# Block totals at the blocks' first positions, and one empty step moved behind level 32, in a gated recurrence on one Trainium2 core

## The chip, the core and the metric

The kernel runs on one core of a Trainium2 chip. The engines of the core have short names in the profile: PE is TensorE, which does the matrix products (PEld is its loading of weights), DVE is VectorE, ACT is ScalarE, POOL is GpSimd, and SP is SyncE, which issues most of the DMAs. The metric is the device time of one execution in microseconds (us), lower is better, as the median of several runs.

## The reference

One layer with a gated linear recurrence (HGRN2), followed by an MLP with a squared ReLU, on 1024 tokens of width 1024 in fp32. The recurrence has 8 heads of width 128. For every head, with gates f, keys k, values v and queries q that come out of one projection:

```python
def step(S, t):                 # S is 128x128 per head
    S = f[t][:, None] * S + k[t][:, None] * v[t][None, :]
    return S, S.T @ q[t]        # o[t]
k = (1 - lb) * sigmoid(-proj_f);  f = lb + (1 - lb) * sigmoid(proj_f)
q = silu(proj_q) / sqrt(128)
x = x + (rmsnorm_per_head(o) * gain * silu(proj_g)) @ w_out
x = x + relu(rmsnorm(x) @ w1) ** 2 @ w2;  out = rmsnorm(x)
```

The reference itself computes the recurrence in chunks of 64 positions, from sums of log f.

## The kernel before

**The products.** Each fp32 operand is split into a high and a low part, and a product of two tiles is three matmuls (L209, L210, L211: high by high, high by low, low by high) that accumulate in PSUM. I call these three a triple. The projections are made for a pair of column blocks at a time by a scheme with seven products in place of eight, from sums of blocks of weights (tiles w..s, split by ACT at L162 and DVE at L163). For each head h there is a `pair` for q and f (j = 0) and one for v and g (j = 1). The last head's second pair is followed by the output projection, whose operands are loaded and split by `fetch` (L805 to L813, with the split at L782 on ACT and L783 on DVE).

**The recurrence in levels.** Within a block of 128 positions the kernel uses no running product in time. It goes by doubling: at level m (1, 2, 4, ..., 64) neighbouring blocks of m positions are joined. The scores between a query of the right block and a key of the left block are a matmul of k and q, which up to then have been multiplied with the gates inside their own blocks. After the matmul of a level three multiplications on DVE carry the tiles to the next level: `carry_q` (L387) multiplies q of the right block with the total gate of the left one, `carry_k` (L394) multiplies k of the left block with the total of the right one, and `carry_f` (L401) makes the total of the joined block. q, k and f are tiles of 128 x 1024; a multiplication touches half of q or k (512 columns), and of f 512 columns at level 1, 256 at level 2, 128 at level 4, and so on.

**The units.** A head's recurrence is a list of steps (L765): `small` (levels 0, 1 and 2: L568, 32 matmuls that read the tile qd made by `prefixes`), `middle` (levels 4 and 8: L601, 32 matmuls that read the tile qe made by `prefixes_2`), `leaf` (level 16: L619), `big` for 32 and for 64 (L649), then kt, vt, kv (the state), `o_unit` (the output, L706 and L708), z (its norm, ACT at L712 and L718), `zt` (transposes, L755) and sums for the output projection. `None` in the list is an empty step. The masked scores are copied out of PSUM by DVE (copy_predicated, L579 to L583 for `small`, L610 for `middle`).

**What sets the order.** The order on PE is the order in which the program is written. In `pair`, after every triple, `pump(650.0)` adds 650 to an account, and whenever that holds `SPACING` (1730, or `LAST_SPACING`, 1800, from the last head's second pair on) the next step of the list is written there, so steps stand two or three triples apart. On DVE, ACT, POOL and SP the tile framework's scheduler sets the order in this part of the program, with a higher priority for the steps of the recurrence (`ahead`: 150, and 400 for the last head). Each engine then works its list in order. The tags in `LEFT` and `NEXT` (L817 to L826) say in which buffers the operands of the output projection are put, and so which earlier use must be over; the key of `LEFT` is the product of the last pair after which they are fetched.

Of the kernel before, what the change touches and what calls it, by code (L numbers as in the profile page):

```python
# [25 lines left out]
ALU = mybir.AluOpType  # L26
# [3 lines left out]
P = 128  # L30
# [9 lines left out]
LEVELS = (1, 2, 4, 8, 16, 32, 64)  # L40
LEAF = 32
SPACING = 1730.0
LAST_SPACING = 1800.0
AHEAD = 6
WARM = 36
WARM_ROW = (6, 6, 6, 4)
# [3 lines left out]
def trunk(ctx: ExitStack, tc: tile.TileContext, x, gains, masks, gfin, w_in, w_out, w1, w2, out):  # L50
    nc = tc.nc
# [197 lines left out]
    with tc.tile_pool(name="scan", bufs=1) as sp:  # L249
# [134 lines left out]
        def halves(a, m):  # L384
            return a.rearrange("p (n two m) -> p n two m", two=2, m=m)

        def carry_q(q, f, m):  # L387

            n = T // (2 * m)
            te = halves(f, m)[:, :, 0, m - 1:m]  # L390
            qo = halves(q, m)[:, :, 1, :]
            nc.vector.tensor_tensor(qo, qo, te.to_broadcast([P, n, m]), ALU.mult)  # L392

        def carry_k(k, f, m):  # L394

            n = T // (2 * m)
            to = halves(f, m)[:, :, 1, m - 1:m]
            ke = halves(k, m)[:, :, 0, :]
            nc.vector.tensor_tensor(ke, ke, to.to_broadcast([P, n, m]), ALU.mult)  # L399

        def carry_f(f, m):  # L401

            fv = halves(f, m)
            te, to = fv[:, :, 0, m - 1:m], fv[:, :, 1, m - 1:m]
            nc.vector.tensor_tensor(to, te, to, ALU.mult)  # L405

        shapes = {"q": ([P, T], 2), "qd": ([P, T // LEAF, 80], 1), "k": ([P, T], 1), "f": ([P, T], 1),
                  "vT": ([P, T], 1), "sg": ([P, T], 1)}
# [128 lines left out]
        def prefixes(tl):  # L537


            q, f, qd = tl["q"], tl["f"], tl["qd"]  # L540
            qb = q.rearrange("p (n l) -> p n l", l=LEAF)
            nc.vector.tensor_tensor(qb, qd[:, :, :LEAF], f.rearrange("p (n l) -> p n l", l=LEAF), ALU.mult)
            nc.scalar.activation(qd[:, :, 32:48], qb[:, :, 1::2], AF.Copy)
            carry_q(q, f, 1)
            q4 = q.rearrange("p (n b j) -> p n b j", b=8, j=4)
            f4 = f.rearrange("p (n b j) -> p n b j", b=8, j=4)
            x1 = qd[:, :, 48:64].rearrange("p n (b j) -> p n b j", j=2)
            x0 = qd[:, :, 64:80].rearrange("p n (b j) -> p n b j", j=2)
            nc.scalar.activation(x1, q4[:, :, :, 2:4], AF.Copy)
            nc.vector.tensor_tensor(x0, q4[:, :, :, 2:4], f4[:, :, :, 1:2].to_broadcast([P, 32, 8, 2]), ALU.mult)  # L550

        def scan_units(h, tl):

# [6 lines left out]
            def small():  # L560
                pss = []
                for g in range(2):
                    ps = psum.tile([P, 4, 80], F32, name=f"lv{h}_0_{g}", tag="s")
                    pss.append(ps)
                    for j in range(4):
                        for b in range(P // LEAF):
                            n = (4 * g + j) * 4 + b
                            nc.tensor.matmul(ps[b * LEAF:(b + 1) * LEAF, j, :], k[:, n * LEAF:(n + 1) * LEAF],  # L568
                                             tl["qd"][:, n, :], start=True, stop=True)
                carry_k(k, f, 1)  # L570
                carry_f(f, 1)
                carry(2)
                prefixes_2()
                m0, m1, m2, m3 = (mk[:, i:i + 1, :] for i in range(4))
                m2, m3 = (m.rearrange("p c (b j) -> p c b j", j=4) for m in (m2, m3))
                for g, ps in enumerate(pss):
                    ac = Ac[:, 4 * g:4 * g + 4, :]
                    a4 = ac.rearrange("p c (b j) -> p c b j", j=4)
                    nc.vector.copy_predicated(ac, m0.to_broadcast([P, 4, LEAF]), ps[:, :, :LEAF])  # L579
                    nc.vector.copy_predicated(ac[:, :, 1::2], m1[:, :, 1::2].to_broadcast([P, 4, 16]), ps[:, :, 32:48])  # L580
                    for i, mm in enumerate((m2, m3)):
                        pv = ps[:, :, 48 + 16 * i:64 + 16 * i].rearrange("p c (b j) -> p c b j", j=2)
                        nc.vector.copy_predicated(a4[:, :, :, 2:4], mm[:, :, :, 2:4].to_broadcast([P, 4, 8, 2]), pv)  # L583

            def prefixes_2():


                qe = st["qe"] = sp.tile([P, T // LEAF, 80], F32, name=f"qe{h}", tag="qd", bufs=1)
                q8 = q.rearrange("p (n b j) -> p n b j", b=4, j=8)
                nc.scalar.activation(qe[:, :, :16].rearrange("p n (b j) -> p n b j", j=4), q8[:, :, :, 4:8], AF.Copy)  # L590
                carry_q(q, f, 4)
                q16, f16 = (a.rearrange("p (n b j) -> p n b j", b=2, j=16) for a in (q, f))
                x1, x0 = (qe[:, :, c:c + 16].rearrange("p n (b j) -> p n b j", j=8) for c in (16, 32))
                nc.scalar.activation(x1, q16[:, :, :, 8:16], AF.Copy)
                nc.vector.tensor_tensor(x0, q16[:, :, :, 8:16], f16[:, :, :, 7:8].to_broadcast([P, 32, 2, 8]), ALU.mult)

            def middle():
                ps = psum.tile([P, NC, 48], F32, name=f"lv{h}_4", tag="s")
                for n in range(T // LEAF):
                    c, b = n // 4, n % 4  # L600
                    nc.tensor.matmul(ps[b * LEAF:(b + 1) * LEAF, c, :], k[:, n * LEAF:(n + 1) * LEAF],  # L601
                                     st["qe"][:, n, :48], start=True, stop=True)
                carry_k(k, f, 4)
                carry_f(f, 4)
                carry(8)
                for i, j, lo in ((4, 4, 0), (5, 8, 16), (6, 8, 32)):
                    odd = [a.rearrange("p c (b two j) -> p c b two j", two=2, j=j)[:, :, :, 1, :]
                           for a in (Ac, mk[:, i:i + 1, :])]
                    pv = ps[:, :, lo:lo + 16].rearrange("p c (b j) -> p c b j", j=j)
                    nc.vector.copy_predicated(odd[0], odd[1].to_broadcast([P, NC, 16 // j, j]), pv)  # L610
                free("qd")

            def leaf(m, i):
                def run():
                    ps = psum.tile([P, NC, LEAF], F32, name=f"lv{h}_{m}", tag="s")
                    for c in range(NC):
                        for b in range(P // LEAF):
                            s = slice(c * P + b * LEAF, c * P + (b + 1) * LEAF)
                            nc.tensor.matmul(ps[b * LEAF:(b + 1) * LEAF, c, :], k[:, s], q[:, s],  # L619
                                             start=True, stop=True)  # L620
                    carry(m)
                    nc.vector.copy_predicated(Ac, mk[:, i:i + 1, :].to_broadcast([P, NC, LEAF]), ps)  # L622
                    if m == LEAF // 2:
                        for b in range(P // LEAF):
                            r = slice(b * LEAF, (b + 1) * LEAF)
                            nc.scalar.activation(AT[r, :, r], Ac[r, :, :], AF.Copy)  # L626
                return run

            def carry(m):

                carry_q(q, f, m)
                carry_k(k, f, m)
                if m == 64:
                    tot = st["tot"] = sp.tile([P, NC], F32, name=f"tot{h}", tag="tot", bufs=2)
                    fv = halves(f, m)
                    nc.vector.tensor_tensor(tot, fv[:, :, 0, m - 1], fv[:, :, 1, m - 1], ALU.mult)
                else:
                    carry_f(f, m)

# [76 lines left out]
            def z_unit():  # L716
                for c in range(NC):
                    nc.scalar.activation(st["z"][:, c, :], st["o"][c // 4][:, c % 4, :], AF.Copy,  # L718
                                         scale=st["r"][:, c:c + 1])
# [29 lines left out]
            def zt():  # L749

                z = tl["sg"]
                for a in range(2):
# [9 lines left out]
                    elif h < last:  # L762
                        nc.sync.dma_start(z_d[h][:, o], z[:, o])

            return (([None] * 4 + [small] + [None] * 2 if h == 0 else [None] * 2 + [small, None, None]) + [middle, None, leaf(16, 7), None]  # L765
                    + [big(32), big(64), None, kt, ("values", h), vt, kv, None, o_unit, lambda: (z_unit(), sums_load()), None, zt, sums_make])

# [35 lines left out]
        def fetch(keys, tags, stages):  # L805

            for i in range(0, len(keys), 2):
# [8 lines left out]
        OPS = [operands(i) for i in range(7)]  # L816
        LEFT = {"b": (OPS[0], ("hT00", "hT01", "hT02", "hT03", "hT04", "hT05"), ("m0", "m1", "m8")),  # L817
                "s2": (OPS[1][:4], ("d4", "d5", "d6", "d7"), ("hT07", "m9")),
                "s1": (OPS[1][4:], ("d0", "d1"), ("m2",)),
                "d": (OPS[2], ("d2", "d3", "d8", "d9", "d10", "d11"), ("m3", "m0", "m1"))}  # L820

        NEXT = {0: (OPS[3], ("hT14", "hT15", "hT16", "hT17", "hT10", "hT11"), ("m2", "m3", "m0")),
                1: (OPS[4], ("hT12", "hT13", "hT00", "hT01", "hT02", "hT03"), ("m1", "m2", "m3")),
                2: (OPS[5] + [("z", 1, 6)], ("hT04", "hT05", "d4", "d5", "d6", "d7", "d10"), ("m0", "m1", "m2", "m3")),
                3: ([("w", 0, 6), ("w", 0, 7), ("w", 1, 6), ("w", 1, 7)] + OPS[6],
# [328 lines left out]
    small = {}  # L1154
# [228 lines left out]
```

## Time and profile before

| | before |
|---|---|
| median of 3 runs | 1138.8 us (1138.57 to 1139.65) |
| the profiled execution | 1139.92 us, its span 1138.1 us |
| PE busy | 1126.3 us, 99% of the span |
| PE weight loads | 931.2 us, 82% |
| DVE busy | 831.2 us, 73% |
| ACT busy | 593.8 us, 52% |
| POOL busy | 40.6 us, 4% |
| granted TensorE clock | 0.999 |
| DMA, mean over the span | 139 GB/s |

The recurrence with its projections takes from about 60 to 480 us of the span, the output projection starts within it, and the MLP takes the rest.

A row of a timeline reads: start in us, duration in us, engine, line of the program, operation, output <- inputs, shape, how many such instructions stand in the row, and in brackets how long the engine had been idle before and what it waited for. Matmuls overlap, and their ends are modelled, so distances between starts say more than durations. A row of the waits reads: engine, what waited, for what, and then the us in total, how often and the longest. The chain that ended last is the sequence of work followed back from the last instruction.

### The profile page before, as it was taken

How to read it: one execution, taken by the hardware profiler on the slowest of the kernel's cores; microseconds unless marked ns; L12 is line 12 of the kernel's file. 1: busy time of each engine (PE TensorE's matmuls, PEld its weight loads, DVE VectorE, ACT ScalarE, POOL GpSimd, SP SyncE). 2: the span in 40 equal slices, each digit the busy share in tenths (PEclk: the TensorE clock that was granted, in tenths of full speed). 3: DMA queues.
4: the chain of work that ended last, by engine and by line, in shares of the span. 5: the costliest groups of instructions: out<-in, count | busy, mean ns of one | idle time of the engine just before them, and what ended most of it. 6: DMA issues, size and time to landing. Idle time of an engine off the chain costs nothing.

```text
span 1138.1 us, 17625 instructions
## 1 busy us (share of the span) xinstructions
PE 1126.3 (99%) x7052; PEld 931.2 (82%) x7052; DVE 831.2 (73%) x1208; ACT 593.8 (52%) x1036; POOL 40.6 (4%) x68
## 2 busy tenths in 40 slices
PE   9999999999999999999999999999999999999997
PEld 7778888887878778888888888888888888888886
DVE  6897888878787889677855664565498755777674
ACT  7756556464645575456664544454553443323552
POOL 1000000000000000010000000000000000000011
PEclk9999999999999999999999999999999999999999
DMA  6113132312223176412244522452798635323331
GB/s 264 38 39 133 62 122 76 112 57 93 75 76 126 55 263 205 150 74 75 93 190 180 203 120 103 185 204 108 259 364 299 206 113 220 113 93 97 126 129 75
DMA packets 48466, 158.58 MB, mean 139 GB/s; under 512 B 5504, under 2 KB 5632, under 8 KB 48384
## 3 DMA queue, kind: packets, MB, share of 16 engines
q1 hardware_dynamic: 47520, 156.26, 38.4%
q8 instruction: 55, 0.90, 0.3%
q10 hardware_dynamic: 864, 1.20, 0.3%
q14 instruction: 27, 0.22, 0.1%
HBM read 109.99 MB, written 47.45 MB: 138 GB/s over the span
## 4 chain that ended last, share of the span: by engine, by line
PE 88%; DVE 5%; ACT 2%; DMA 2%; issue 1%; POOL 1%; POOLq 0%; ACTq 0%; DVEq 0%
PE m1X L210 5%; PE m1X L211 5%; PE m1X L209 5%; PE m2X L209 5%; PE m2X L211 5%; PE m2X L210 5%; PE pX L209 4%; PE pX L211 3%; PE pX L210 3%; PE m1Y L210 3%; PE m2Y L209 3%; PE m1Y L211 3%; PE m1Y L209 3%; PE m2Y L211 3%; PE m2Y L210 3%; PE pY L209 2%
## 5 line engine op out<-in xcount | busy, mean ns | idle before, releaser
L993 ACT ACTIVATE a<-ai 128x1024 fp32r<-128x1024 f32 x56 | 58.9, 1052 | 71.4 <-PE m2X L210 28.3
L994 DVE TENSOR_TENSOR a<-ai,a 128x1024 fp32r<-128x1024 f32 x56 | 68.3, 1219 | 11.1 <-ACT a L993 11.1
L1095 ACT ACTIVATE e<-e 128x1024 f32<-128x1024 f32 x24 | 25.5, 1062 | 72.5 <-DVE e L1142 72.5
L1172 DVE TENSOR_TENSOR acc<-acc,m2X 128x512 f32<-128x512 f32 x32 | 21.1, 685 | 34.3 <-PE m2X L211 34.2
L392 DVE TENSOR_TENSOR q<-q,f 128x512 f32<-128x512 f32 x56 | 38.4, 687 | 2.2 <-PE lv L649 2.2
L399 DVE TENSOR_TENSOR k<-k,f 128x512 f32<-128x512 f32 x56 | 38.3, 684 | 0.0
L1092 ACT ACTIVATE e<-e 128x1024 f32<-128x1024 f32 x32 | 34.0, 1062 | 1.0
L626 ACT ACTIVATE AT<-Ac 32x256 f32<-32x256 f32 x32 | 13.3, 415 | 35.3 <-DVE Ac L622 35.1
L145 DVE TENSOR_TENSOR raw<-raw,raw 128x512 f32<-128x512 f32 x42 | 29.0, 689 | 0.8
L718 ACT ACTIVATE z<-o,rs_z 128x128 f32<-128x128 f32 x64 | 17.4, 384 | 17.8 <-POOL rs_z L115 17.8
L1123 ACT ACTIVATE e<-m1X 128x512 f32<-128x512 f32 x30 | 16.9, 593 | 17.2 <-PE m1X L211 17.2
L706 PE MATMUL o<-v,AT 128*128 128x128 f32 x128 | 23.4, 275 | 0.0
L114 POOL TENSOR_SCALAR rs_f<-fs 128x1 f32<-128x1 f32 x4 | 2.1, 531 | 570.5 <-ACT ot L1176 570.5
L1172 DVE TENSOR_TENSOR acc<-acc,m2Y 128x512 f32<-128x512 f32 x16 | 10.8, 686 | 15.4 <-PE m2Y L211 14.7
L708 PE MATMUL o<-S,q 128*128 128x128 f32 x112 | 21.7, 275 | 0.0
L1142 DVE TENSOR_TENSOR e<-e,m1Y 128x512 f32<-128x512 f32 x16 | 10.9, 686 | 14.2 <-PE m1Y L211 14.2
L706 PEld LDWEIGHTS o<-v,AT 128*128 128x128 f32 x128 | 19.4, 191 | 0.6
L405 DVE TENSOR_TENSOR f<-f 128x512 f32<-128x512 f32 (+5 forms) x48 | 19.0, 396 | 0.1
L693 DVE SCALAR_TENSOR_TENSOR S<-S,tot,kv 128x128 f32<-128x128 f32 x48 | 16.7, 347 | 2.0
L114 POOL TENSOR_SCALAR rs_z<-zs 128x8 f32<-128x8 f32 x8 | 3.7, 458 | 390.1 <-ACT z L712 390.1
L708 PEld LDWEIGHTS o<-S,q 128*128 128x128 f32 x112 | 17.0, 192 | 0.0
L712 ACT ACTIVATE z<-o 128x128 f32<-128x128 f32 x64 | 16.7, 284 | 0.1
(1843 smaller groups left out, 3886.4 us busy)
## 6 DMA issues: line engine op xcount, KB each, us to landing
raw<-in_w_in SPq DMA_DIRECT2D x32, 512.0 KB, 3.6
ai<-adt SPq DMA_DIRECT2D x32, 512.0 KB, 4.4
adB<-e SPq DMA_DIRECT2D x24, 512.0 KB, 2.6
adt<-t SPq DMA_DIRECT2D x24, 512.0 KB, 4.3
ai<-adB SPq DMA_DIRECT2D x24, 512.0 KB, 4.5
izs<-sd SPq DMA_DIRECT2D x21, 256.0 KB, 3.3
x<-in_x SPq DMA_DIRECT2D x8, 512.0 KB, 7.1
xr<-in_x SPq DMA_DIRECT2D x8, 512.0 KB, 5.5
```

Of the source, the lines that this page charges most:

```text
L145: nc.vector.tensor_tensor(out_, a, b, ALU.add)
L209: nc.tensor.matmul(ps, lhi, rhi, start=start, stop=False, **more)
L210: nc.tensor.matmul(ps, lhi, rlo, start=False, stop=False, **more)
L211: nc.tensor.matmul(ps, llo, rhi, start=False, stop=stop, **more)
L392: nc.vector.tensor_tensor(qo, qo, te.to_broadcast([P, n, m]), ALU.mult)
L399: nc.vector.tensor_tensor(ke, ke, to.to_broadcast([P, n, m]), ALU.mult)
L706: nc.tensor.matmul(ps[:, j, :], AT[:, c, :], v[:, c, :], start=True, stop=c == 0)
L708: nc.tensor.matmul(ps[:, j, :], q[:, c * P:(c + 1) * P], st["S"][:, c - 1, :], start=False, stop=True)
L993: nc.scalar.activation(hi, x, AF.Copy)
L994: nc.vector.tensor_tensor(lo, x, hi.bitcast(F32), ALU.subtract)
L1092: nc.scalar.activation(t, t, AF.Square)
L1172: nc.vector.tensor_tensor(t, t, ps, op)
```

## The change

The total gate of a block is now kept at the block's first position; it was kept at its last one. With it at the last one, `carry_f` of a level overwrites the total of the right block, which `carry_k` of the same level still has to read, and so f of a level had to wait for k of that level. With it at the first one, `carry_f` overwrites the total of the left block, which `carry_q` of the level reads and `carry_k` does not. In the program, f of level 1, q of level 2 and f of level 2 move from behind the matmuls of `small` into `prefixes`; f of level 4, q of level 8 and f of level 8 move from `middle` into `prefixes_2`. The multiplications of k stay behind the matmuls that read k. No instruction is added or removed, and shapes stay the same.

One empty step between `small` and `middle` is taken out and one is put between `big(32)` and `big(64)` (the last head keeps its two ahead of `middle`). `LAST_SPACING` goes from 1800 to 1700. Three groups of operands of the output projection are put in other buffers, and one of them is fetched after another product.

```diff
-LAST_SPACING = 1800.0
+LAST_SPACING = 1700.0
         def carry_q(q, f, m):
-            te = halves(f, m)[:, :, 0, m - 1:m]
+            te = halves(f, m)[:, :, 0, 0:1]
         def carry_k(k, f, m):
-            to = halves(f, m)[:, :, 1, m - 1:m]
+            to = halves(f, m)[:, :, 1, 0:1]
         def carry_f(f, m):
-            te, to = fv[:, :, 0, m - 1:m], fv[:, :, 1, m - 1:m]
-            nc.vector.tensor_tensor(to, te, to, ALU.mult)
+            te, to = fv[:, :, 0, 0:1], fv[:, :, 1, 0:1]
+            nc.vector.tensor_tensor(te, te, to, ALU.mult)
         def prefixes(tl):
...
+            carry_f(f, 1)
+            carry_q(q, f, 2)
+            carry_f(f, 2)
             def small():
...
                 carry_k(k, f, 1)
-                carry_f(f, 1)
-                carry(2)
+                carry_k(k, f, 2)
                 prefixes_2()
             def prefixes_2():
...
+                carry_f(f, 4)
+                carry_q(q, f, 8)
+                carry_f(f, 8)
             def middle():
...
                 carry_k(k, f, 4)
-                carry_f(f, 4)
-                carry(8)
+                carry_k(k, f, 8)
-            return (([None] * 4 + [small] + [None] * 2 if h == 0 else [None] * 2 + [small, None, None]) + [middle, None, leaf(16, 7), None]
-                    + [big(32), big(64), None, kt, ...
+            return (([None] * 4 + [small, None] if h == 0 else [None] * 2 + [small] + [None] * (2 if h == last else 1)) + [middle, None, leaf(16, 7), None]
+                    + [big(32), None, big(64), None, kt, ...
         LEFT = {...
-                "s1": (OPS[1][4:], ("d0", "d1"), ("m2",)),
-                "d": (OPS[2], ("d2", "d3", "d8", "d9", "d10", "d11"), ("m3", "m0", "m1"))}
-        NEXT = {0: (OPS[3], ("hT14", "hT15", "hT16", "hT17", "hT10", "hT11"), ("m2", "m3", "m0")),
+                "s3": (OPS[1][4:], ("d8", "d9"), ("m2",)),
+                "d": (OPS[2], ("d10", "d11", "hT14", "hT15", "hT16", "hT17"), ("m3", "m0", "m1"))}
+        NEXT = {0: (OPS[3], ("d0", "d1", "d2", "d3", "hT10", "hT11"), ("m2", "m3", "m0")),
```

Where the groups stand on PE, counted in triples between them:

| from, to | before | changed |
|---|---|---|
| small to middle, heads 0 to 5 | 8 | 5 |
| small to middle, head 6 | 8 | 6 |
| small to middle, head 7 | 9 | 8, and small itself one earlier |
| middle to leaf(16), heads 0 to 2 | 5 | 6 |
| middle to leaf(16), heads 3, 4, 5 and 7 | 5 | 5 |
| middle to leaf(16), head 6 | 6 | 5 |
| leaf(16) to big(32) | 5 or 6 | 5 or 6 |
| big(32) to big(64) | 2 or 3 | 5 or 6 |
| kt and all behind it, heads 0 to 6 | | same place |
| vt, the output and zt, head 7 | | one triple earlier |

On DVE, in head 6, between the first mask copies of `small` and qe (L595 before, L597 changed). q_3575, k_3742 and f_3743 are the head's tiles, lv_0_0 and lv_0_1 the two PSUM tiles of `small`; L399 is a multiplication of k, L405 of f, L392 of q. Before:

```order
L399 TENSOR_TENSOR k_3742<-k_3742,f_3743 128x512
L583 COPY_PREDICATED Ac<-mk,lv_0_0_3988 128x32x2
L405 TENSOR_TENSOR f_3743<-f_3743 128x512
L579 COPY_PREDICATED Ac<-mk,lv_0_1_4005 128x128
L392 TENSOR_TENSOR q_3575<-q_3575,f_3743 128x256x2
L399 TENSOR_TENSOR k_3742<-k_3742,f_3743 128x256x2
L580 COPY_PREDICATED Ac<-mk,lv_0_1_4005 128x64
L405 TENSOR_TENSOR f_3743<-f_3743 128x256
L583 COPY_PREDICATED Ac<-mk,lv_0_1_4005 128x32x2
L392 TENSOR_TENSOR q_3575<-q_3575,f_3743 128x128x4
L583 COPY_PREDICATED Ac<-mk,lv_0_1_4005 128x32x2
L595 TENSOR_TENSOR qe_4027<-q_3575,f_3743 128x32x16
```

With the change, at the same place:

```order
L399 TENSOR_TENSOR k_3742<-k_3742,f_3743 128x512
L585 COPY_PREDICATED Ac<-mk,lv_0_0_3991 128x32x2
L399 TENSOR_TENSOR k_3742<-k_3742,f_3743 128x256x2
L392 TENSOR_TENSOR q_3575<-q_3575,f_3743 128x128x4
L581 COPY_PREDICATED Ac<-mk,lv_0_1_4008 128x128
L597 TENSOR_TENSOR qe_4027<-q_3575,f_3743 128x32x16
L405 TENSOR_TENSOR f_3743<-f_3743 128x128
L582 COPY_PREDICATED Ac<-mk,lv_0_1_4008 128x64
L392 TENSOR_TENSOR q_3575<-q_3575,f_3743 128x64x8
```

Two multiplications of f and one of q are gone from between k and qe, three mask copies now stand behind qe, and f of level 4 (128x128) follows qe at once.

On ACT, in head 7, around the two copies into qe (L590 and L594 before, L592 and L596 changed). sig_4549 and sig_4629 (sig_4543 and sig_4632 changed) are the sigmoids of the gate's two halves, the oz.. and ow.. tiles are splits for the output projection. Before:

```order
L444 ACTIVATE sig_4549<-e_4524 128x512
L590 ACTIVATE qe_4600<-q_4123 128x32x16
L782 ACTIVATE oza_4804<-iza_4801 128x512
L444 ACTIVATE sig_4629<-pX_4363 128x512
L594 ACTIVATE qe_4600<-q_4123 128x32x16
L782 ACTIVATE owB_4807<-iza_4801 128x512
```

With the change:

```order
L444 ACTIVATE sig_4543<-e_4527 128x512
L786 ACTIVATE owB_4650<-izs_4644 128x512
L592 ACTIVATE qe_4597<-q_4123 128x32x16
L786 ACTIVATE ozs_4656<-izs_4653 128x512
L786 ACTIVATE owB_4659<-izs_4653 128x512
L596 ACTIVATE qe_4597<-q_4123 128x32x16
L786 ACTIVATE oza_4828<-iza_4825 128x512
L444 ACTIVATE sig_4632<-pX_4366 128x512
```

Both copies into qe now stand ahead of the split oza, which needs a load, and of the second sigmoid.

On DVE, in head 7, from the addition to vT to the multiplication of k of level 8, with the change (sg_4542 is the gate, whose second half needs sig_4632):

```order
L145 TENSOR_TENSOR vT_4413<-vT_4413,pY_4514 128x512
L582 COPY_PREDICATED Ac<-mk,lv_0_1_4578 128x64
L448 TENSOR_TENSOR sg_4542<-sig_4632,pX_4366 128x512
L585 COPY_PREDICATED Ac<-mk,lv_0_1_4578 128x32x2
L787 TENSOR_TENSOR owB_4650<-izs_4644,owB_4650 128x512
L585 COPY_PREDICATED Ac<-mk,lv_0_1_4578 128x32x2
L399 TENSOR_TENSOR k_4286<-k_4286,f_4287 128x128x4
L614 COPY_PREDICATED Ac<-mk,lv_4_4688 128x32x4
L399 TENSOR_TENSOR k_4286<-k_4286,f_4287 128x64x8
```

Before, the same addition, gate and split stood ahead of k of level 4 too, but behind the qe for which PE waits, and f of level 4 and q of level 8 stood between the two multiplications of k.

More of the change, by code (lines that the diff above doesn't have):

```diff
@@ L594, in prefixes_2 @@
                 nc.scalar.activation(x1, q16[:, :, :, 8:16], AF.Copy)
-                nc.vector.tensor_tensor(x0, q16[:, :, :, 8:16], f16[:, :, :, 7:8].to_broadcast([P, 32, 2, 8]), ALU.mult)
+                nc.vector.tensor_tensor(x0, q16[:, :, :, 8:16], f16[:, :, :, 4:5].to_broadcast([P, 32, 2, 8]), ALU.mult)
+                carry_f(f, 4)
+                carry_q(q, f, 8)
+                carry_f(f, 8)
             def middle():
@@ L635, in carry @@
                     fv = halves(f, m)
-                    nc.vector.tensor_tensor(tot, fv[:, :, 0, m - 1], fv[:, :, 1, m - 1], ALU.mult)
+                    nc.vector.tensor_tensor(tot, fv[:, :, 0, 0], fv[:, :, 1, 0], ALU.mult)
                 else:
@@ L763, in zt @@
                         nc.sync.dma_start(z_d[h][:, o], z[:, o])
-            return (([None] * 4 + [small] + [None] * 2 if h == 0 else [None] * 2 + [small, None, None]) + [middle, None, leaf(16, 7), None]
-                    + [big(32), big(64), None, kt, ("values", h), vt, kv, None, o_unit, lambda: (z_unit(), sums_load()), None, zt, sums_make])
+            return (([None] * 4 + [small, None] if h == 0 else [None] * 2 + [small] + [None] * (2 if h == last else 1)) + [middle, None, leaf(16, 7), None]
+                    + [big(32), None, big(64), None, kt, ("values", h), vt, kv, None, o_unit, lambda: (z_unit(), sums_load()), None, zt, sums_make])
         OUT = (("Z", "b", "B21", 0, 0, ALU.add), ("Y", "s1", "t1", 1, 1, ALU.subtract), ("Y", "s4", "B22", 0, 1, ALU.add),
```

## The prediction

> **What bounds the kernel now.** I read the busy line of the page first, then what TensorE (PE) waits for, then the timelines around those waits.
>
> ```profile
> PE 1126.3 (99%) x7052; PEld 931.2 (82%) x7052; DVE 831.2 (73%) x1208; ACT 593.8 (52%) x1036; POOL 40.6 (4%) x68
> ```
>
> PE is never idle for long, and the change adds and removes no instruction on any engine. So it can only act on the times in which PE stands still. The Trainium skill (Perfetto Trace Analysis, Identifying the Most-Contended Engine) says that the matmul busy share is no good measure of headroom and that the weight-load share is; by its 82% some 207 us would be free, and the distances between starts below show a few us of waiting in the recurrence, so the trace does not bear out a gain of that size.
>
> The list of waits names the recurrence three times:
>
> ```profile
> PE lv L601 <- DVE qe L595: 1.3, 3, 0.8
> PE lv L601 <- ACT qe L594: 0.9, 1, 0.9
> PE pY L209 <- ACT e L526: 0.3, 1, 0.3
> ```
>
> L601 is the group of 32 matmuls of the levels 4 and 8 ("middle"). It reads qe, which is the last link of a chain of multiplications on VectorE (DVE). Ends of matmuls are modelled, so I measure from the start of the last L211 to the start of L601. In head 2 nothing is waited for:
>
> ```profile
> 170.24 0.39 PE L211 MATMUL pX<-h0B,w6a 128*128 128x512 f32 x1
> 170.56 0.44 PE L601 MATMUL lv<-qe,k 128*32 128x48 f32 x21
> ```
>
> That is 0.32. In heads 0, 4, 6 and 7 it is more:
>
> ```profile
> 68.24 0.39 PE L211 MATMUL pX<-h0B,w2a 128*128 128x512 f32 x1
> 68.85 0.55 PE L601 MATMUL lv<-qe,k 128*32 128x48 f32 x33 [0.23 <-DVE qe L595]
> ...
> 271.62 0.39 PE L211 MATMUL pX<-h0B,w10a 128*128 128x512 f32 x1
> 272.27 0.53 PE L601 MATMUL lv<-qe,k 128*32 128x48 f32 x30 [0.26 <-DVE qe L595]
> ...
> 372.56 0.39 PE L211 MATMUL pX<-h0B,w14a 128*128 128x512 f32 x1
> 373.74 0.46 PE L601 MATMUL lv<-qe,k 128*32 128x48 f32 x25 [0.80 <-DVE qe L595]
> ...
> 425.94 0.39 PE L211 MATMUL oZ<-owB,ozb 128*128 128x512 f32 x1
> 427.21 0.59 PE L601 MATMUL lv<-qe,k 128*32 128x48 f32 x36 [0.89 <-ACT qe L594]
> ```
>
> The distances are 0.61, 0.65, 1.18 and 1.27, so 0.29, 0.33, 0.86 and 0.95 are waiting, 2.4 in all. Two waits of other kinds lie near by. The transposes zt of z (L755) take 1.03 in head 6, and more in heads 7 and 0, because their operand comes piece by piece:
>
> ```profile
> 104.06 1.57 PE L755 MATMUL zt<-ident,z 128*128 128x128 f32 x8
> ...
> 409.64 1.03 PE L755 MATMUL zt<-ident,z 128*128 128x128 f32 x8
> ...
> 465.12 1.65 PE L755 MATMUL zt<-ident,z 128*128 128x128 f32 x8
> ```
>
> That is 0.62 in head 7 and 0.54 in head 0.
>
> **The chain on DVE, and what leaves it.** Head 6, from the first mask copy after the small levels to qe:
>
> ```profile
> 367.78 0.30 DVE L579 COPY_PREDICATED Ac<-mk,lv 128x128 f32<-128x128 uint8 x1
> ...
> 369.32 0.69 DVE L405 TENSOR_TENSOR f<-f 128x512 f32<-128x512 f32 x1
> ...
> 370.12 0.69 DVE L392 TENSOR_TENSOR q<-q,f 128x512 f32<-128x512 f32 x1
> 370.72 0.68 DVE L399 TENSOR_TENSOR k<-k,f 128x512 f32<-128x512 f32 x1
> 371.32 0.29 DVE L580 COPY_PREDICATED Ac<-mk,lv 128x64 f32<-128x64 uint8 x1
> 371.45 0.62 DVE L405 TENSOR_TENSOR f<-f 128x256 f32<-128x256 f32 x1
> 371.98 0.28 DVE L583 COPY_PREDICATED Ac<-mk,lv 128x64 f32<-128x64 uint8 x1
> 372.17 0.69 DVE L392 TENSOR_TENSOR q<-q,f 128x512 f32<-128x512 f32 x1
> ...
> 372.91 0.68 DVE L595 TENSOR_TENSOR qe<-q,f 128x512 f32<-128x512 f32 x1
> ```
>
> From 367.78 to the end of qe at 373.59 are 5.81 us; PE starts 0.15 later. The change takes f of level 1, q of level 2 and f of level 2 out of this stretch: 0.60 + 0.60 + 0.53 = 1.73 by the pitch of the starts. Mask copies that filled in between them go behind qe as well: in the new order of head 6 five of the eight stand ahead of qe instead of all eight; from such a copy to the next start are 0.13 (371.32) to 0.19 (371.98), so three make about 0.47. The chain gets shorter by 1.73 + 0.47 = 2.20.
>
> In return PE comes earlier. One triple of matmuls of the projection lasts 3 x 0.227 = 0.68 us by the starts of L209, L210 and L211 (0.22 to 0.24 apart), and from the small group to the middle one there are 8 triples before. With the change there are 5 in heads 0 to 5 (PE is 2.04 earlier), 6 in head 6 (1.36), and in head 7 one triple less behind a small group that itself starts one triple earlier (1.36). What remains of the waits is the old wait, plus PE's lead, minus the chain's 2.20: head 0: 0.29 + 2.04 - 2.20 = 0.13 (its order keeps f of level 2 in the chain, but only one mask copy, which comes to nearly the same); head 4: 0.17; head 6: 0.86 + 1.36 - 2.20 = 0.02. Heads 1 to 3 waited for nothing, and the chain gains 0.16 more than PE does, so nothing appears there. Gains: 0.16, 0.16 and 0.84.
>
> **Where the 1.73 us go.** They are put behind the last prefix operation of a head (L550), while the products ahead of the small group still run. There DVE stands idle:
>
> ```profile
> 156.19 0.69 DVE L163 TENSOR_TENSOR w6s<-raw,w6s 128x512 fp32r<-128x512 f32 x1 [2.12 <-ACT w6s L162]
> ...
> 164.48 0.30 DVE L579 COPY_PREDICATED Ac<-mk,lv 128x128 f32<-128x128 uint8 x1 [0.50 <-PE lv L568]
> ...
> 359.21 0.69 DVE L163 TENSOR_TENSOR w14s<-raw,w14s 128x512 fp32r<-128x512 f32 x1 [2.86 <-ACT w14s L162]
> ...
> 410.56 0.69 DVE L783 TENSOR_TENSOR ozb<-izb,ozb 128x512 fp32r<-128x512 f32 x1 [2.75 <-ACT ozb L782]
> ```
>
> Idle stretches of 2.12 (head 2), 2.86 (head 6) and 2.75 (head 7) each hold 1.73, and in head 2 DVE even waits for PE again at the small group (0.50). So I cost the moved work at nothing. Without that cover it would cost up to 1.73 a head (the third rival). What it delays meanwhile are the weight splits w..s, which PE needs several triples later.
>
> **Head 7.** Here the chain ends on ScalarE (ACT), and PE also waits for the copy e:
>
> ```profile
> 415.77 0.58 ACT L526 ACTIVATE e<-pY 128x512 f32<-128x512 f32 x1
> ...
> 415.74 0.39 PE L211 MATMUL pX<-ht,w15s 128*128 128x512 f32 x1
> 416.40 0.50 PE L209 MATMUL pY<-h0B,w15s 128*128 128x512 f32 x1 [0.27 <-ACT e L526]
> ...
> 425.52 0.63 ACT L782 ACTIVATE oza<-iza 128x512 fp32r<-128x512 f32 x1 [0.94 <-DMA iza<-zd]
> 426.06 0.58 ACT L444 ACTIVATE sig<-pX 128x512 f32<-128x512 f32 x1
> ```
>
> In the new order three of ACT's splits that stood ahead of e stand behind it, 3 x 0.52 = 1.56 earlier for e, and the wait in front of pY (0.66 - 0.23 = 0.43) goes. The copy of q into qe now stands ahead of oza and sig, so the middle group no longer waits for them and its 0.95 go. But something new is late next. DVE's gate multiplication waits for sig (ends 426.64) and now stands ahead of both multiplications of k, which the group of level 16 (L619) reads: 426.64 + 0.60 (gate) + 0.13 + 0.60 (a split) + 0.13 + 0.60 (k, level 4) + 0.13 + 0.69 (k, level 8) = 429.52, and with 0.15 PE could start at 429.67. How long PE takes from middle to level 16 is shown by head 1, which has five triples there as head 7 has now:
>
> ```profile
> 120.01 0.49 PE L601 MATMUL lv<-qe,k 128*32 128x48 f32 x26
> ...
> 124.45 0.34 PE L619 MATMUL lv<-q,k 128*32 128x32 f32 x17
> ```
>
> 4.44. PE reaches the middle of head 7 at 425.94 + 0.32 - 1.36 - 0.43 = 424.47 and level 16 at 428.91. A new wait of about 0.75 stands there. Its bounds are 0 (the load lands 0.8 earlier) and 2.5 (second rival). Head 7 gives 0.95 + 0.43 - 0.75 = 0.63.
>
> The same question in head 6: behind qe's new end at 371.4 come two f, one q, an addition, a gate, two k and five mask copies, by the pitches above some 4.1 us, while PE arrives 4.44 after the middle group; 0.3 are left, so nothing is counted.
>
> **The transposes.** In head 7 ACT stands in front of the z pieces for 2.36 us until a load of izd lands:
>
> ```profile
> 458.78 0.63 ACT L782 ACTIVATE ozd<-izd 128x512 fp32r<-128x512 f32 x1 [2.36 <-DMA izd<-zd]
> ```
>
> Now the z pieces come first and this split behind them. z is then ready more than 1 us earlier, and zt comes 0.68 earlier: the 0.62 go. In head 0 the sums' load goes ahead of two weight loads and may bring z earlier; the bounds are 0 and 0.54, and since no row of this run shows the new order I take the middle, 0.27. Behind the recurrence the listed waits of PE hold nothing that could take such a gain back, so a shift made in heads 0 to 7 reaches the end.
>
> **Sum.** 0.16 + 0.16 + 0.84 + 0.63 + 0.62 + 0.27 = 2.68. The profiled execution took 1139.92 (span 1138.1 and 1.8 around it) and would take 1137.2; it lies 1.1 above the median of the three runs, so for the median 1138.8 - 2.7 = **1136.1**. About 0.2% (2.3 us) is what a measurement of this kernel can tell from no change, so faster begins at 1136.5.
>
> **The rivals.**
>
> 1. All waits go: what I left standing (0.13 + 0.17 + 0.02 in the middle groups, 0.75 at level 16, 0.27 at zt) goes too, 1.3 more: 1134.8. For it: a mask copy or a split less in a row is enough for the small ones. Against it: the load of iza sets the 0.75, and nothing moves it forward.
>
> 2. The wait goes to k. The load behind head 7's 0.75 has this row in the chain that ended last:
>
> ```profile
> 417.32 0.29 DVE ozs L783
> 417.61 7.89 DMA iza<-zd
> ```
>
> It is issued when DVE has finished a split (ozs) for the buffer. If f and q of head 7 push that split back by the whole 1.73, level 16 waits 0.75 + 1.73 = 2.5, and the 0.3 of head 6 is used up by the same push (up to 1.4 of it without cover). With head 7 alone the time is 1136.1 + 1.7 = 1137.8, no change that can be told. For it: in every head from 4 on, the multiplications of k now stand behind two additions. Against it: the 2.75 idle at 410.56.
>
> 3. Slower: DVE is too full ahead of the small group. Its idle stretches are waits for ACT's split; if ACT is held up by DVE in turn (the copy of q at L549, the splits of the raw weights), the moved operations shift all that follows on DVE, and the first mask copy is late by a backlog b in each of heads 1 to 6. The middle then waits longer by b in heads 4 to 6 and by b less 0.2 in heads 1 to 3: 6b - 0.6. It is slower than before from 6b - 0.6 = 2.7 on, b = 0.55, a third of 1.73. With half of 1.73 uncovered the time is 1136.1 + 4.6 = 1140.7. Against it: the idle stretches quoted. For it: PE has given up 2.04 of distance and has none left.
>
> 4. The change does not shorten the chain, because the scheduler keeps the old place of the operations: the order excludes that, so it gets no chance.
>
> **How the numbers follow.** Chances: my forecast 0.48, rival 1 0.14, rival 2 0.27, rival 3 0.11. The forecast's own range goes from 1135.4 to 1136.8: 0.27 either way for zt of head 0, and 0.43 for the runs, which lay 1.1 us apart. Some 0.44 of its 0.48 lies below 1136.5. Faster: 0.44 + 0.14 = 0.58; slower 0.09 of rival 3's 0.11; the remaining 0.33 is within 0.2%. The range for 8 in 10 takes in rivals 1 and 2: 1134.6 to 1138.6.
>
> **What would show it.** Right: L601 starts 0.3 to 0.5 after the last L211 in all heads; qe ends 3.6 after the first mask copy; pY without a wait; L619 of head 7 waits 0.5 to 1 for k; zt of head 7 about 1.0. Wrong: idle before L601 of 0.5 or more in heads 1 to 5 with the first mask copy later than 0.9 after the small group's start (rival 3); waits at L619 of head 7 over 1.5, or any in heads 3 to 6 (rival 2); a landing of iza far from 425.5; a PE wait behind 480 that before has not.

## The result and the profile after

The changed kernel takes 1145.95 us (median of 6 runs, 1145.26 to 1146.35), the kernel before on the same chip 1139.7 (median of 6). The ratio is 1.0056, with a 95% interval of 1.0043 to 1.0069: slower by 6.3 us, where 2.7 us less were forecast. The profiled execution's span is 1144.2 us, 6.1 more than the 1138.1 of before. The time was lost at a place that the prediction never looked at for a loss.

The busy line of the page after:

```profile
PE 1132.2 (99%) x7052; PEld 931.8 (81%) x7052; DVE 831.2 (73%) x1208; ACT 594.1 (52%) x1036; POOL 50.6 (4%) x68
```

DVE and ACT are busy as long as before (831.2; 593.8 and 594.1). POOL, which has the same 68 instructions, is busy 10 us longer: 40.6 before, 50.6 now. The groups of instructions between 60 and 490 us show which (line, engine, operation, tiles, shape, how many | busy us, mean ns | idle before). Of before:

```profile
L114 POOL TENSOR_SCALAR rs_z<-zs 128x8 f32<-128x8 f32 x8 | 3.7, 458 | 390.1 <-ACT z L712 390.1
```

Of after, with the transposes that follow from it:

```profile
L114 POOL TENSOR_SCALAR rs_z<-zs 128x8 f32<-128x8 f32 x8 | 13.7, 1707 | 385.1 <-ACT z L716 385.1
L759 PE MATMUL zt<-ident,z 128*128 128x128 f32 x64 | 15.1, 316 | 1.1 <-ACT z L722 1.1
```

L114 adds a constant to 8 sums of squares per row, on 128 x 8 elements: the first of two POOL operations in the norm of z. It takes 1707 ns on the mean, and took 458. Behind it stand POOL's power (L115), ACT's scaling of z (L722) and then zt on PE. One head in the timelines of after (POOL, DVE, ACT, PE):

```profile
359.89 2.19 POOL L114 TENSOR_SCALAR rs_z<-zs 128x8 f32<-128x8 f32 x1 [48.29 <-ACT z L716]
362.16 1.66 POOL L115 TENSOR_TENSOR rs_z<-rs_z,neghalf 128x8 f32<-128x8 f32 x1
...
358.96 0.68 DVE L405 TENSOR_TENSOR f<-f 128x512 f32<-128x512 f32 x1
359.57 0.68 DVE L145 TENSOR_TENSOR raw<-raw 128x512 f32<-128x512 f32 x1
360.17 0.68 DVE L392 TENSOR_TENSOR q<-q,f 128x512 f32<-128x512 f32 x1
360.77 0.68 DVE L145 TENSOR_TENSOR raw<-raw,raw 128x512 f32<-128x512 f32 x1
361.37 0.61 DVE L405 TENSOR_TENSOR f<-f 128x256 f32<-128x256 f32 x1
361.89 0.69 DVE L145 TENSOR_TENSOR vT<-vT,pZ 128x512 f32<-128x512 f32 x1
...
363.86 1.92 ACT L722 ACTIVATE z<-o,rs_z 128x128 f32<-128x128 f32 x7 [4.05 <-POOL rs_z L115]
...
363.73 0.39 PE L211 MATMUL pX<-ht,w13s 128*128 128x512 f32 x1
364.28 2.14 PE L759 MATMUL zt<-ident,z 128*128 128x128 f32 x8 [0.16 <-ACT z L722]
366.17 0.48 PE L209 MATMUL pY<-ht,w13s 128*128 128x512 f32 x1
```

The scheduler put the three moved operations (L405, L392, L405) between the two sums of raw weights, with no gap between any two of the five. All five read two operands from SBUF. POOL starts L114 at 359.89, in the middle of them, and ends it at 362.08: 0.10 after the last of them (361.37 + 0.61), when DVE already runs the addition that takes one operand from PSUM (pZ). The same place in the kernel before:

```profile
354.12 0.58 POOL L114 TENSOR_SCALAR rs_z<-zs 128x8 f32<-128x8 f32 x1 [48.41 <-ACT z L712]
...
353.91 0.69 DVE L145 TENSOR_TENSOR raw<-raw,raw 128x512 f32<-128x512 f32 x1
355.66 0.69 DVE L145 TENSOR_TENSOR vT<-vT,pZ 128x512 f32<-128x512 f32 x1 [1.06 <-PE pZ L211]
```

Here DVE's row of sums ends at 354.60, L114 ends at 354.70, and DVE is idle for 1.06 us. This pause ahead of the addition is where POOL got its turn. It is not the idle stretch that the prediction offered as cover for this head: that one, 2.86 us up to 359.21, lies behind the addition. The moved operations never reached it. They stand ahead of the addition, where they fill the short pause and make the row longer, and in after the long stretch is still there, longer than before:

```profile
366.58 0.69 DVE L163 TENSOR_TENSOR w14s<-raw,w14s 128x512 fp32r<-128x512 f32 x1 [4.01 <-ACT w14s L162]
```

The other two quoted stretches grew as well: from 2.12 to 3.42 ahead of w6s in head 2, from 2.75 to 3.08 ahead of ozb in head 7.

On PE this shows in the distance from the last L211 ahead of zt to the L209 behind it: 366.17 - 363.73 = 2.44, and 1.02 where nothing is waited for. The middle groups did what was forecast (heads 6 and 7 of after):

```profile
378.40 0.39 PE L211 MATMUL pX<-ht,w13d 128*128 128x512 f32 x1
378.92 0.29 PE L606 MATMUL lv<-qe,k 128*32 128x48 f32 x7
...
430.83 0.39 PE L211 MATMUL oZ<-owB,ozb 128*128 128x512 f32 x1
431.15 0.34 PE L606 MATMUL lv<-qe,k 128*32 128x48 f32 x12
```

0.52 and 0.32 instead of 1.18 and 1.27. And at level 16 of head 7 a new wait stands (ACT, DVE and PE of after):

```profile
432.75 0.63 ACT L786 ACTIVATE oza<-iza 128x512 fp32r<-128x512 f32 x1 [3.22 <-DMA iza<-zd]
433.29 0.58 ACT L444 ACTIVATE sig<-pX 128x512 f32<-128x512 f32 x1
...
433.90 0.69 DVE L448 TENSOR_TENSOR sg<-sig,pX 128x512 f32<-128x512 f32 x1 [1.23 <-ACT sig L444]
...
435.27 0.39 PE L211 MATMUL oZ<-owB,ozb 128*128 128x512 f32 x1
437.00 0.39 PE L623 MATMUL lv<-q,k 128*32 128x32 f32 x24 [1.34 <-DVE k L399]
```

All distances of this kind on PE, summed as differences between after and before:

| place | forecast, us | measured, us |
|---|---|---|
| middle groups, heads 0 to 7 | -2.11 | -2.07 |
| pY of head 7 | -0.43 | -0.43 |
| level 16 of head 7 | +0.75 | +1.41 |
| zt of head 7 | -0.62 | -0.62 |
| zt of head 0 | -0.27 | +0.96 |
| zt of heads 1 to 6 | 0 | +1.43, 1.43, 1.16, 1.43, 1.42, 0.25 = +7.12 |
| sum | -2.68 | +6.37 (spans: +6.1) |

### The profile page after: what moved, and what is told of

Its sections match the earlier page's. It is cut to its first block, busy times and chain, and to the rows that moved or that the text cites. A ratio compares the mean times of both kernels' runs of the same rounds, so it can differ in the third digit from the quotient of the medians.

```text
span 1144.2 us, 17636 instructions
## 1 busy us (share of the span) xinstructions
PE 1132.2 (99%) x7052; PEld 931.8 (81%) x7052; DVE 831.2 (73%) x1208; ACT 594.1 (52%) x1036; POOL 50.6 (4%) x68
## 4 chain that ended last, share of the span: by engine, by line
PE 90%; ACT 3%; POOL 3%; DVE 2%; DMA 1%; issue 1%; POOLq 0%; ACTq 0%; DVEq 0%
PE m1X L209 5%; PE m1X L210 5%; PE m1X L211 5%; PE m2X L211 5%; PE m2X L210 5%; PE m2X L209 5%; PE pX L209 4%; PE pX L211 4%; PE pX L210 4%; PE m1Y L209 3%; PE m2Y L211 3%; PE m1Y L210 3%; PE m2Y L210 3%; PE m2Y L209 3%; PE m1Y L211 3%; PE pY L209 2%
## 5 line engine op out<-in xcount | busy, mean ns | idle before, releaser
L392 DVE TENSOR_TENSOR q<-q,f 128x512 f32<-128x512 f32 x56 | 38.6, 690 | 3.2 <-PE lv L653 2.9
L399 DVE TENSOR_TENSOR k<-k,f 128x512 f32<-128x512 f32 x56 | 38.5, 687 | 0.0
L722 ACT ACTIVATE z<-o,rs_z 128x128 f32<-128x128 f32 x64 | 17.4, 383 | 28.4 <-POOL rs_z L115 28.4
L114 POOL TENSOR_SCALAR rs_z<-zs 128x8 f32<-128x8 f32 x8 | 13.7, 1707 | 385.1 <-ACT z L716 385.1
L114 POOL TENSOR_SCALAR rs_f<-fs 128x1 f32<-128x1 f32 x4 | 2.1, 529 | 570.5 <-ACT ot L1180 570.5
L405 DVE TENSOR_TENSOR f<-f 128x512 f32<-128x512 f32 (+5 forms) x48 | 19.1, 398 | 0.0
L519 ACT ACTIVATE q<-pX 128x512 f32<-128x512 f32 x14 | 8.4, 599 | 17.5 <-PE pX L211 17.3
```

## The experiments

Theory A: POOL's two small operations cannot read their operands while DVE runs one operation on SBUF operands after the other, and zt waits for them. Theory B: DVE has too much work ahead of the small groups (the prediction's third rival). All eight kernels were compared with the kernel before; its median was 1139.46 in both sets of runs, and the ratios are to it.

### The three operations in a step of their own, behind the addition to vT

```diff
         def prefixes(tl):
-            carry_f(f, 1)
-            carry_q(q, f, 2)
-            carry_f(f, 2)
+            def early():     # a step in place of the None ahead of small
+                with tc.issue_after(tl["add"]) if h else ExitStack():
+                    carry_f(f, 1)
+                    carry_q(q, f, 2)
+                    carry_f(f, 2)
```

`issue_after` queues them on DVE behind the addition of pZ to vT.

> The changed kernel, but f of level 1, q of level 2 and f of level 2 are queued on VectorE behind the addition of pZ to vT (in heads 1 to 7), in a step of their own in place of an empty one; the arithmetic is the same. Theory A (GpSimd's two small operations for the norm of z cannot read while VectorE runs one operation with two SBUF operands after the other, so L114 takes 2.2 us instead of 0.3 to 0.8 and zt waits): L114 is back at 0.3 to 0.8, the step from the last L211 to the L209 behind zt at 1.0 to 1.5 instead of 2.45 in heads 1 to 6, and the time 7 us below the changed kernel, 1137 to 1139. Theory B (VectorE has too much work ahead of the small group, rival 3): the three operations now stand later and nearer to the small group, so the time stays at 1146 or rises.

Measured: 1140.02, ratio 1.0005 (0.9996 to 1.0014): 6 us below the change and no different from before. L114:

```profile
L114 POOL TENSOR_SCALAR rs_z<-zs 128x8 f32<-128x8 f32 x8 | 3.7, 463 | 389.2 <-ACT z L721 389.2
```

The mean is back at 463 ns, and zt takes 1.02 in heads 1 to 7 and 1.17 in head 0. That is theory A's place and size. Yet it stayed above what A alone gives, because the middle groups wait again, 1.03 in each of heads 4 to 6 and 0.44 in head 3. In DVE's timeline of head 6 the reason can be read:

```profile
357.32 0.69 DVE L405 TENSOR_TENSOR f<-f 128x512 f32<-128x512 f32 x1
360.25 0.69 DVE L163 TENSOR_TENSOR w14s<-raw,w14s 128x512 fp32r<-128x512 f32 x1 [2.25 <-ACT w14s L162]
360.86 0.69 DVE L392 TENSOR_TENSOR q<-q,f 128x512 f32<-128x512 f32 x1
```

Only the first of the three stands ahead of the split for which DVE waits 2.25 us; q of level 2 and f of level 2 stand behind it, and push all that follows. In heads 4 to 6 the first mask copy comes 0.83 to 0.85 later behind the small group than in the change (2.81 against 1.98 in head 6). So the backlog of theory B is real where the operations stand late in DVE's list. It just isn't what happened in the change.

### Scratch products early, in the kernel before

```diff
+            for i in range(3):     # end of prefixes
+                nc.vector.tensor_tensor(dummy, q[:, i * 128:i * 128 + 512], f[:, :512], ALU.mult)
```

> The kernel before, with three more VectorE operations per head behind the last prefix operation: products of q and f into a scratch tile that nothing reads (two SBUF operands, 512 columns). Nothing else changes. Theory A: L114 takes about 2.2 us in heads 1 to 6, zt waits 1.2 to 1.5 longer in heads 1 to 6 and about 0.8 in head 0, and the time is 1138.8 + 8 = 1146 to 1148. Theory B (only VectorE's backlog counts): the 1.8 us fit into the idle time of 2 to 3 us behind them, so the time stays within 1 us of before.

Measured: 1148.44, ratio 1.0083 (1.0067 to 1.0098), 9 us slower.

```profile
L114 POOL TENSOR_SCALAR rs_z<-zs 128x8 f32<-128x8 f32 x8 | 14.2, 1770 | 387.5 <-ACT z L718 387.5
L761 PE MATMUL zt<-ident,z 128*128 128x128 f32 x64 | 15.1, 316 | 1.7 <-ACT z L724 1.7
```

Three products that nobody reads give the same signature as the change: L114 at 2.27 in most heads, zt at 316 ns as in the change, the step around zt at 2.5 to 2.65 in heads 1 to 5 instead of 1.02 (1.28 in head 3). The program differs in nothing else. From 125 to 410 us, where these five heads lose 7.4 us, PE, ACT and POOL run what they ran before in the same order, and so does DVE but for the scratch products and two operations on the sums (jS) that come later. So it is shown that such DVE operations at this place make L114 long and zt late.

### Scratch products late

The same products in a step ahead of `small`, queued behind the addition to vT.

> The kernel before with the same three scratch products, but queued behind the addition of pZ to vT, when GpSimd's first operation is over. Theory A: L114 as before (0.3 to 0.8), zt as before, the time within 1.5 us of before. Theory B: the same work on VectorE, nearer to the small group, so at least as slow as with the products early.

Measured: 1145.99, ratio 1.0058 (1.0044 to 1.0072). Both expectations missed. L114 is at 474 ns on the mean and zt at 278 ns, as A said, but the time is not near before. The loss has moved to the middle groups:

```profile
PE lv L609 <- DVE qe L603: 5.0, 4, 1.9
PE lv L609 <- ACT qe L602: 2.5, 1, 2.5
```

7.5 us of waiting there, 2.2 before. In heads 4 to 6 the first mask copy comes 1.08 to 1.15 later than before, and the chain of 5.8 behind it has no slack there, so the late place costs on DVE what the early place costs through POOL. Heads 2 and 3 wait for nothing; head 7 waits for ACT's copy into qe, which was not traced further.

### Scratch operations with one operand

```diff
-            for i in range(3):
-                nc.vector.tensor_tensor(dummy, q[:, i * 128:i * 128 + 512], f[:, :512], ALU.mult)
+            for i in range(4):
+                nc.vector.tensor_scalar(dummy, q[:, i * 128:i * 128 + 512], 0.5, None, op0=ALU.mult)
```

> The kernel before with four scratch operations per head that have one SBUF operand each (q times a constant), at the place of the early products. Theory A with the port held only by operations with two SBUF operands: GpSimd gets in between them, L114 stays below 1.5 us and the loss is below 3 us. If any VectorE operation on SBUF holds it: L114 2 us and more and a loss of about 8 us.

Measured: 1146.56, ratio 1.0066 (1.0053 to 1.008). L114 takes 1.15 us on the mean, between the 0.46 of before and the 1.77 of the products with two operands, and 1.47 to 1.68 in heads 1 to 5. So neither case of the expectation came out: L114 lies about the bound of 1.5 in those heads, and the loss is near the 8 us of the other case. Of the 7 us, 4.6 are lost at zt; the middle groups wait longer as well, 3.9 in all and 2.2 before, most of it in head 0. POOL and DVE around one L114:

```profile
359.73 1.67 POOL L114 TENSOR_SCALAR rs_z<-zs 128x8 f32<-128x8 f32 x1 [48.53 <-ACT z L718]
...
360.28 0.69 DVE L145 TENSOR_TENSOR raw<-raw,raw 128x512 f32<-128x512 f32 x1
360.88 0.42 DVE L556 TENSOR_SCALAR dummy<-q 128x512 bf16<-128x512 f32 x1
361.34 0.43 DVE L556 TENSOR_SCALAR dummy<-q 128x512 bf16<-128x512 f32 x1
```

L114 ends at 361.40, which is 0.10 after the end of the third scratch operation (361.30), as elsewhere it ends 0.10 after an operation with two operands. Between the third and the fourth DVE leaves a gap of 0.03; all the others in the row start before the one ahead has ended. A single scratch operation at 359.95, between two sums, did not let L114 in, and neither did the third while it ran. This is so in each of heads 1 to 5. So an operation with one SBUF operand held POOL off too, and it was the gap that let it in. L114 is shorter than with the products because the gap came earlier: the scratch operations are shorter here, 0.33 us from start to start in place of 0.60.

### The block totals alone

The change with the list of steps, `LAST_SPACING` and the buffers of before.

> The change of the block totals alone: empty steps, the last spacing and the buffers of the operands as before. Theory A: L114 takes about 2.2 us, zt waits 1.4 longer in heads 1 to 6 as in the whole change, nothing waits at the middle groups, and the time is 1138.8 - 2.7 + 7.5 = 1143.6 (1142.5 to 1145.5). If the moved empty step or the buffers cost the time, it is 1136 to 1137.

Measured: 1148.95, ratio 1.0084 (1.0071 to 1.0098). The loss at zt is there as expected (2.45 in heads 1 to 5) and the middle groups wait for nothing. The expectation was 5 us too low, most of it because level 64 now waits:

```profile
133.53 0.69 PE L653 MATMUL lv<-q,k 128*64 128x64 f32 x16 [1.14 <-DVE f L405]
```

Its waits are 0.44, 1.21, 1.21 and 0.98 in heads 0, 1, 2 and 7. In the whole change, with an empty step behind `big(32)`, level 64 waits for nothing; that this step is what removes the wait was not run by itself. A wait at level 64 was not in the prediction at all.

### The places alone

The kernel before with the list of steps, `LAST_SPACING` and the buffers of the change.

> The places alone: the empty steps, the last spacing and the buffers of the change, with the block totals and the chain of the kernel before. The chain from the first mask copy to qe takes 5.8 us and PE comes 2.04 earlier (1.36 in heads 6 and 7): the middle groups wait 1.8 in heads 1 to 3 and 2.2 to 2.4 in the others, 16 to 17 in all instead of 2.7, and the time is 1138.8 + 14 = 1153 (1151 to 1155); zt and L114 as before. If the shorter chain was not needed for the earlier place, 1139 to 1141.

Measured: 1158.37, ratio 1.0168 (1.0154 to 1.0182). The middle groups wait 17.1 us in all, as expected:

```profile
PE lv L601 <- DVE qe L595: 8.7, 4, 2.3
PE lv L601 <- ACT qe L594: 7.8, 4, 2.3
```

(16.5 by the idle time, 17.1 by starts.) zt is at 1.02 everywhere and L114 at 498 ns, so the places alone do not bring POOL's delay. The other 5 us are the clock (see the last section); the four times spread from 1156.98 to 1160.37, at granted clocks of 0.995 to 0.991. With the run before this one it shows that neither half gains alone: the chain without the places costs 9.5 us, the places without the chain 19, both together 6.3. Of the chain's 9.5, however, 7.1 are the loss at zt, which the whole change has too; what the places take away is the 3.8 at level 64, and they add 1.0 at level 16 of head 7.

### One swap on ACT

In the change, the splits of iza on ACT, oza first, are queued behind the second sigmoid of head 7 (its instruction is kept under "sig").

```diff
-                fetch(*NEXT[i])
+                with tc.issue_after(heads[last]["sig"]) if i == 0 else ExitStack():
+                    fetch(*NEXT[i])
```

> The changed kernel with one swap: on ScalarE the second sigmoid of head 7 stands ahead of the split oza, which waits for a load. If the chain load, oza, sigmoid, gate, split, k, k sets the wait of 1.4 at the level 16 group of head 7, that wait falls below 0.3 and the time is 1146.0 - 1.3 = 1144.7. If k is late for another reason (VectorE's own queue), the wait stays above 1.

Measured: 1144.88 (ratio 1.0048, 1.0033 to 1.0063), 1.1 below the change. The interval overlaps with that of the change, so the timeline decides:

```profile
430.33 0.60 ACT L444 ACTIVATE sig<-pX 128x512 f32<-128x512 f32 x1 [0.44 <-PE pX L211]
433.44 0.63 ACT L786 ACTIVATE oza<-iza 128x512 fp32r<-128x512 f32 x1 [2.51 <-DMA iza<-zd]
...
435.64 0.39 PE L211 MATMUL oZ<-owB,ozb 128*128 128x512 f32 x1
435.96 0.43 PE L623 MATMUL lv<-q,k 128*32 128x32 f32 x28
```

The sigmoid runs 3 us ahead of the load, and level 16 starts 0.32 after the last L211. The chain from the load to k is shown to set that wait.

### Both mended

The three operations right behind the addition to vT and ahead of the next weight split, and the swap on ACT.

```diff
                         add(dst, dst, p_)
+                        if j == 1 and m == "b":
+                            with tc.high_priority(150), tc.issue_after(ins.ins):
+                                marks[h] = totals(tl)      # f of level 1, q of level 2, f of level 2
...
-            nc.vector.tensor_tensor(w[:, 1], src, w[:, 0].bitcast(F32), ALU.subtract)
+            with tc.issue_after(marks[n // 2 - 1]) if m == "s1" and n % 2 == 0 and n // 2 - 1 in marks else ExitStack():
+                nc.vector.tensor_tensor(w[:, 1], src, w[:, 0].bitcast(F32), ALU.subtract)
```

> The changed kernel with f of level 1, q of level 2 and f of level 2 behind the addition of pZ to vT, all three ahead of the first weight split that follows it (the split that VectorE waited 2 to 2.9 us for in the kernel before), and with head 7's second sigmoid ahead of the split oza on ScalarE. Theory A (GpSimd must get its two operations in, and the three operations must lie in VectorE's idle time): L114 at 0.6 or less, zt at 1.0 in all heads, the middle groups wait 0.2 at most in heads 1 to 6, and the level 16 group of head 7 waits less than 0.3; the time is 1138.8 - 2.1 - 0.4 - 1.2 = 1135 (1134.5 to 1136.5), below both kernels. Theory B (the later place costs at the middle groups whatever follows): waits of 0.4 to 1.0 there as in the run with the step of its own, 1138 to 1140.

Measured: 1135.95 (1135.75 to 1136.5), ratio 0.9971 (0.996 to 0.9982): 3.5 us below the kernel before and 10 below the change. DVE of head 6, and the group of POOL:

```profile
354.49 0.69 DVE L146 TENSOR_TENSOR vT<-vT,pZ 128x512 f32<-128x512 f32 x1 [1.06 <-PE pZ L213]
355.10 0.69 DVE L407 TENSOR_TENSOR f<-f 128x512 f32<-128x512 f32 x1
355.89 0.69 DVE L394 TENSOR_TENSOR q<-q,f 128x512 f32<-128x512 f32 x1
356.61 0.63 DVE L407 TENSOR_TENSOR f<-f 128x256 f32<-128x256 f32 x1
358.03 0.69 DVE L165 TENSOR_TENSOR w14s<-raw,w14s 128x512 fp32r<-128x512 f32 x1 [0.79 <-ACT w14s L163]
...
L114 POOL TENSOR_SCALAR rs_z<-zs 128x8 f32<-128x8 f32 x8 | 3.7, 461 | 384.6 <-ACT z L726 384.6
```

All three lie in the idle time, 0.79 of which is left; POOL keeps the 1.06 ahead of the addition, and zt takes 1.02 in heads 1 to 7. Of the waits in the middle groups 0.21 is left in one head, of that at level 16 0.28. With the two losses taken away, the kernel gains 3.5 us, where 2.7 were forecast for the change; that the time itself, 1135.95, is so near the forecast 1136.1 is in part luck, because the kernel before measured 1139.46 in this set and 1138.8 when the forecast was made. The gain has other parts too: zt lost its wait of 0.26 in head 3, which the forecast does not have, and level 16, with the swap, waits 0.28 and not 0.75.

## Why the prediction was wrong

**Right: the chain and the middle groups.** The chain from the first mask copy to qe is 3.63 us in head 6 of after (375.15 to 378.78), forecast 3.61. The gain at the middle groups of all heads is 2.07, forecast 2.11, though spread a little differently: all of head 0's 0.29 went, and 0.20 instead of 0.02 was left in head 6. Head 5, which the prediction left out, waited 0.18 before and after.

**Right in mechanism, off in size: level 16 of head 7.** The chain load, oza, sigmoid, gate, split, two k is the one that was named, and the swap shows it. It was mis-sized: 1.41 for 0.75, as the load landed later against PE (the split oza could start only at 432.75, 1.6 after the middle group began at 431.15; forecast were 425.52 against 424.47, 1.05). The load was issued 6.46 ahead of the middle group instead of 6.86 and took 8.04 instead of 7.89.

**Wrong: "So I cost the moved work at nothing".** This step under "Where the 1.73 us go" took the long idle stretches of DVE as the place of the moved operations, and looked only at what they delay in DVE's own queue. Both failed. The operations did not get to those stretches: they stand ahead of the addition to vT, in heads 1 to 6 in a row of sums, and the stretches are longer than before. And the step did not ask who else needs the short pause that they filled: POOL's L114 had to wait for the end of the row. The scratch products show that operations at that place cost through POOL. At zt the change loses 8.1 us in heads 0 to 6, three times the forecast gain. The cover itself was real: in the last kernel the same three operations lie in the stretch that was quoted for head 6, with 0.79 us to spare, and the loss is gone.

The Trainium skill (GPSIMD Engine Reference, Specifications) states that GpSimd's SBUF interfaces are shared with VectorE, with contention when VectorE runs instructions with two SBUF inputs or in a 2-port mode. The traces here agree for two inputs: L114 goes from 0.6 to 2.2 us. In which mode the scratch operations with one operand ran, no run here shows.

**Wrong in the same way: head 0's zt.** The sums' load went ahead of the weight loads, as assumed, and L114 started earlier. But it took 2.04 us, and the forecast gain of 0.27 became a loss of 0.96. In the two kernels in which L114 is short there (0.32 and 0.29, with the operations behind the addition), zt takes 1.17: a gain of 0.39, inside the bounds of 0 and 0.54.

**The third rival had the side and not the cause.** The first mask copy comes 0.83 after the small group in head 2 of after, as before; in heads 0 to 4 nothing changed there, and in heads 5 to 7 it is 0.14, 0.17 and 0.29 later, well under the 0.55 a head that this rival needed. The backlog appears when the same work is moved late instead.

**The first rival** (all waits go) is what the last kernel nearly shows, at 1135.95; the second (k late) appeared in head 7 alone, and at 1.41 instead of its 2.5.

The row that could have warned stood in the trace of before: L114 took 0.24 to 0.26 in four heads and 0.58 to 0.79 in the other four, for the same 128 x 8 elements, and in the long ones it ended 0.10 after DVE's row of sums did. And zt of head 3, which the prediction does not list, already took 1.28: L114 ended 0.30 later there than in head 2, counted from the start of the output group, and zt waited 0.26. So the chain through POOL had almost no slack.

## What to carry to other kernels

An operation that is moved towards an engine's idle time isn't free until one knows two things: whether the scheduler really puts it into the stretch that was counted on, and who uses the pauses that it fills on the way. List the short operations of POOL around the new place, and look whether their time already varies with what DVE does. A chain that is made shorter and a consumer that is moved up belong together and should be costed each alone too: here the chain alone loses 3.8 us at level 64, and the places alone 14.5 at the middle groups. Where a scheduler picks the place, tie the moved work to the instruction behind which the idle time begins, and tie what waits at its end behind the work.

## What the runs showed of the hardware

Two things were not expected. A POOL operation on 128 x 8 elements of SBUF, 0.24 to 0.79 us before, took 2.2 us with DVE operations on two SBUF operands back to back around it; the next one (L115) kept its 1.66 us while DVE ran the addition with a PSUM operand. In the traces of the two kernels and the eight runs, L114 takes over 0.3 us 59 times. Each time it ends 0.09 to 0.12 us after the end of a DVE operation, and in all but one behind that operation DVE was idle, left a gap of 0.03 us, or went on with the addition from PSUM. (The one is head 0 with the block totals alone, where a product of two SBUF operands was already running.) So here a row of DVE operations on SBUF held POOL up to the row's first gap, and 0.03 us of gap was enough.

And a wait of PE can cost more than its length. With the places alone, PE waited 2.14 us for the middle group of head 4; then the clock in that stretch was 0.67 (columns: stretch, us, PE busy and count, granted clock, DMA share, GB/s), and the matmuls started 0.427 apart instead of 0.227 until 288.6:

```profile
286.00:290.00 4.00, 4.00 (x13) 0.67 0.49 131
...
284.08 0.89 PE L601 MATMUL lv<-qe,k 128*32 128x48 f32 x64 [2.14 <-DVE qe L595]
...
286.12 0.63 PE L209 MATMUL pX<-h0B,w10a 128*128 128x512 f32 x1
286.55 0.63 PE L210 MATMUL pX<-h0B,w10a 128*128 128x512 f32 x1
```

This happened in five of the eight heads of that kernel, after waits of 1.9 to 2.3 us, 8 or 9 matmuls each, 8 us in all. It is what its 1158 has above the expected 1153 (the shorter zt gives some of it back). In the other three heads waits of the same length (1.92 to 2.33) left the matmuls at 0.227. The late scratch products show the same: 8 matmuls at 0.427 after the wait of 2.02 in head 6, none after 2.54 in head 7. What tells these cases apart was not tried.
